# A two-layer diffusion backbone on one core: prescribed TensorE order at three places, unread products in two waits, later norm transposes inside the projection

## The chip, the cores and the metric

The kernel runs as one program on one core of one Trainium2 chip. The metric is device microseconds of one execution; a figure for a kernel is the median over several executions. PE is TensorE (PEld its weight loads), DVE is VectorE, ACT is ScalarE, POOL is GpSimd, SP is SyncE.

## The reference, cut to what matters

The kernel takes 512 latent tokens of width 1024 and 256 context tokens through two layers. Layer 0 mixes by attention and a Fourier transform, layer 1 by a conformer convolution; both end in a gated FFN with a small convolution. Each part is preceded by an RMS norm that is modulated by shift and scale vectors computed from the condition `c`.

```python
sh1, sc1, g1, sh2, sc2, g2 = ada_params(c, w_ada[i], b_ada[i])   # silu(c) @ w + b
h_lat = modulate(rmsnorm(x_lat, g_mix[i]), sh1, sc1)
o_lat, _ = hybrid_mixer(h_lat, h_ctx, ...)      # layer 0
o_lat = conformer_conv(h_lat, ...)              # layer 1: glu, dwconv 31, layernorm, silu, @ w_pw2
x_lat = x_lat + g1 * o_lat
h = modulate(rmsnorm(x_lat, g_ffn[i]), sh2, sc2)
x_lat = x_lat + g2 * conv_ffn(h, w_up[i], w_fdw[i], b_fdw[i], w_down[i])
```

All of it is float32. The kernel writes each operand as a high and a low part, and each product of two matrices as three TensorE products (high by high, low by high, high by low).

## The kernel before, in words

**Products.** `mm3` issues the three products (L224, L225, L226). Weights come in chunks of 128x1024: a transfer into `st`, ACT casts the high part `whi` (L196), DVE subtracts it for the low part `wlo` (L197). `Stream` holds five such pairs and two `st`; all transfers of this part are issued by SP in program order.

**Order.** The program text is handed to a scheduler that fixes one order for each engine before the program runs. On the chip every engine works through its own list in that order, so an instruction that waits holds up all behind it on the same engine. `issue_after(ins)` tells the scheduler that what follows may stand only behind `ins` on its list.

**Projection of layer 0 (`load_and_project`).** The input features come in eight groups `kt` of 128. For each, `modulate(kt)` makes `tmp = xnT * modA + modS` on DVE (L561), ACT casts the high part of `h` (L290), DVE subtracts the low one (L291). Then PE adds 12 products of 128x256 into the key/value accumulators (two banks, B) and 12 of 128x512 into the query accumulators (D). `modS` and `modA` come from the condition, two feature groups (a quarter) at a time: `Quarter.product` (L383, eight products with 32 output rows), a copy out of the bank by ACT (L385), and `Quarter.columns` (L391, four products that turn rows into columns). The quarter for `kt` 2 and 3 stands in the text behind `kt` 0 (product) and `kt` 1 (columns), and so on. From `kt` 4 on the context's parts are added (`hc`, L566 on ACT), and `project(0)` starts the Fourier branch (24 products of 128x512 into another bank).

**Heads (`heads_and_fourier`).** When the key/value sums are complete, ACT copies and squares them (L695, L696), DVE reduces, POOL takes a root (L287), DVE scales and rotates, PE transposes; the same for four tiles of queries.

**Attention.** For each tile of 128 queries and key/value group, four score products per head (L813), maximum on DVE (L815), exponential on ACT (L818), transposes (L830) and products with the values (L835). `fill()` runs one step of a filler: the condition's products for later parts (`Block.product`, L340), sixteen PE records in a half block.

**Tails.** In each FFN the last two chunks of the down projection are added for four token tiles `t`; then `residual` (L455, L456 on DVE), and, if a norm follows, `fin(t)`: square sum (ACT L485), root (DVE, POOL), scaling (DVE L487), and for a pair of tiles the transposes `features` (PE L472), shift and scale (ACT L477) and the split of `h` (DVE L479, L480). The next part begins with products over the first 256 tokens (`first_blocks`).

**End of the conformer.** After the fourth quarter of the convolution's inverse transform, DVE sums up the layer norm's statistics and normalises four tiles `ytm` (L1203); PE transposes them feature group by feature group (L1207, eight groups of four), ACT and DVE make `h`, and `token_major("pw2", ...)` multiplies.

Of the kernel before, what the change touches and what calls it, by code (L numbers as in the profile page):

```python
# [17 lines left out]
P = 128  # L18
# [203 lines left out]
def mm3(nc, out, lhs, rhs, start, stop):  # L222
    (lh, ll), (rh, rl) = lhs, rhs
    nc.tensor.matmul(out, lhsT=lh, rhs=rh, start=start, stop=False)  # L224
    nc.tensor.matmul(out, lhsT=lh, rhs=rl, start=False, stop=False)  # L225
    nc.tensor.matmul(out, lhsT=ll, rhs=rh, start=False, stop=stop)  # L226


@with_exitstack
def tile_hybrid_backbone(ctx: ExitStack, tc: tile.TileContext, x_in, ctx_in, vecs_in, gains_in, cond_in, condT_in, wada, wnat,  # L230
# [124 lines left out]

    turn = []

    def in_turn(dst, src):

        with tc.issue_after(turn[-1]) if turn else nullcontext():  # L360
            turn.append(nc.sync.dma_start(dst, src).ins)

    class Quarter:

# [13 lines left out]
        def product(self):  # L378
            g = bank()
            kts = range(KT) if self.qd == 0 else (6, 7, 4, 5, 2, 3, 0, 1)  # L380
            for n, kt in enumerate(kts):
                o = 32 * (kt % 4)
                nc.tensor.matmul(g[o : o + 32, :], lhsT=cT[:, kt, :], rhs=self.st[kt // 2][:, kt % 2, :], start=n < 4, stop=n >= 4)  # L383
            self.gs = tmp()
            nc.scalar.copy(self.gs, g)  # L385

        def columns(self):

            b = bank()
            for k in range(4):  # L390
                nc.tensor.matmul(b[:, 2 * k : 2 * k + 2], lhsT=self.gs[:, k * P : (k + 1) * P], rhs=sel, start=True, stop=True)  # L391
            return b[:, 0:8].rearrange("p (j k r) -> p j k r", j=2, k=2)

    def in_every_row(col, dst, halves=(0, 1)):
# [41 lines left out]
    def chain(*gens):  # L436
        for g in gens:
            yield from g
# [86 lines left out]
    def load_and_project(gain, keep, pre):  # L525
# [21 lines left out]
                else:  # L547
                    nc.vector.tensor_copy(o, i)

        def modulation(cols):  # L550

            raw = cols.columns()
# [46 lines left out]
        quarters[1].load(4)  # L599
        for t in range(TT):  # L600
            x_rows(t)
        quarters[0].product()
        modulation(quarters[0])
        stream.fill(3)
        quarters[2].load(4)
# [16 lines left out]
        for kt in range(KT):  # L622
            modulate(kt)
            stream.fill()
            wq = stream.get(("q", kt // 2))
            wk = stream.get(("kv", kt // 4))
            rq = tuple(w[:, (kt % 2) * 512 : (kt % 2 + 1) * 512] for w in wq)
            rk = rks[kt] = tuple(w[:, (kt % 4) * 256 : (kt % 4 + 1) * 256] for w in wk)
            if kt == 0:
                for kb in (K0, K1):  # L630
                    nc.tensor.matmul(kb, lhsT=zero, rhs=rq[0], start=True, stop=False)
            for t in range(TT):
                mm3(nc, kv_ps[t], hsl(h, kt, t * P, (t + 1) * P), rk, False, kt == KT - 1 and t % 2 == 1)
            for t in range(TT):
                mm3(nc, q_ps[t], hsl(h, kt, t * P, (t + 1) * P), rq, kt == 0, kt == KT - 1)
            if kt % 2 == 0 and kt < 6:
                quarters[kt // 2 + 1].product()
            if kt == 0:
                quarters[3].load(4)
            if kt % 2 == 1 and kt < 6:  # L640
                modulation(quarters[kt // 2 + 1])
            if kt == 3:
                for t in range(2):
                    ctx_rows(xcs[t], t)
                rope = chunk_tile()[:, 0:512].rearrange("p (a t d) -> p a t d", a=2, t=TT)
# [156 lines left out]
    def attention(qT, kk, vv, ap, fill):  # L802
        units = [(t, kv) for t in range(TT) for kv in range(NKV)]

        def scores(t, kv):
            ps_ = []
            for g in range(GRP):
                hd = kv * GRP + g
                s = bank2()
                lq = qT[:, hd, t * P : (t + 1) * P]  # L810
# [71 lines left out]
    def mixer():  # L882
        A2, S2 = mods[0]
        with ExitStack() as tables:
# [4 lines left out]
            with sbuf("qkv") as qkv:  # L889
# [6 lines left out]
                with sbuf("att") as ap:  # L896
# [21 lines left out]
                    filler = sums()  # L918
                    run(filler)

                    def fill():
                        stream.fill(stream.loaded + next(ahead))
                        run(filler)

                    attention(qT, kk, vv, ap, fill)
# [5 lines left out]
    def ffn(l, filler, filler1, mods, out_dram=None):  # L931
        nd = NF // 2
        with sbuf(nm("ff")) as fp:
# [88 lines left out]
                fin = finisher(fp, *mods)  # L1022
            gs = [gsplit(2 * (nd - 2) + i) for i in range(4)]
            ws = [stream.get(("dn", l, 1, nd - 2 + i)) for i in range(2)]
            for t in range(TT):
                for i in range(4):
                    mm3(nc, acc[t], tuple(u[:, t * P : (t + 1) * P] for u in gs[i]), tuple(u[:, (i % 2) * 512 : (i % 2 + 1) * 512] for u in ws[i // 2]), False, i == 3)
                residual(t, 1, acc[t], gate2, out_dram)
                if t == TT - 1:
                    for i in range(2):  # L1030
                        stream.release(("dn", l, 1, nd - 2 + i))
                if mods is not None:
                    fin(t)


    def conformer(filler, mods):
        with sbuf("cf") as cf, ExitStack() as inner:
# [57 lines left out]
            def conv_quarter(q):  # L1095
# [43 lines left out]
                def inverse(pt, bt):  # L1139
                    if bt == 0:  # L1140
                        mm3(nc, acc[pt], tuple(u[:, 4, pt * P : (pt + 1) * P] for u in iv), zs[0], True, False)
                    for o in range(2):
                        mm3(nc, acc[pt][:, o * 256 : o * 256 + 256], tuple(u[:, 2 * o + bt, pt * P : (pt + 1) * P] for u in iv),
                            tuple(u[:, o * 256 : o * 256 + 256] for u in zs[1 + bt]), False, bt == 1 and o == 1)

                for z in ((0, 0), (1, 0), (0, 1), (1, 1)):
                    inverse(*z)
                for pt in range(2):
                    ys = tmp(256)
                    nc.scalar.copy(ys, acc[pt][:, 256:512])  # L1150
# [164 lines left out]
```

## Time and profile before

| | |
|---|---|
| Median of 3 executions | 1201.29 us (1201.06 to 1203.15) |
| The profiled execution | 1202.3 us, of which the span of the core is 1200.5 us |
| Busy share of the span | PE 96 %, PEld 80 %, DVE 64 %, ACT 43 %, POOL 9 % |
| Mean granted clock of TensorE | 0.99 of full speed |

The span runs from the first to the last instruction; 1.8 us lie around it. A granted clock of 1.00 is the level of 2.4 GHz, 0.50 that of 1.2 GHz. Idle time is written behind the instruction that ended it, with the releaser.

### The profile page before, as it was taken

Reading aid. Unit: us, or ns where it says so; the run is one execution under the profiler, and the core shown is the slowest. Engines: PE = TensorE matmul, PEld = TensorE weight load, DVE = VectorE, ACT = ScalarE, POOL = GpSimd, SP = SyncE. Lnnn points to the kernel's source line nnn. Section 1 sums busy time; section 2 is a strip of 40 time slices with the busy share of each in tenths; the row PEclk is TensorE's granted clock in tenths of the full one; section 3 lists DMA queues with packets and bytes.
Section 4 is the critical chain, followed back from the end, with each engine's and each line's share of the span. In section 5 each row is a group of like instructions: output and inputs, shape, how many; then the busy total and the mean of one; then the engine's idle time right before and its main releaser. Section 6 shows DMA issues by size and latency. Waiting matters only on the chain.

```text
span 1200.5 us, 15245 instructions
## 1 busy us (share of the span) xinstructions
PE 1158.5 (96%) x5849; PEld 963.6 (80%) x5849; DVE 769.6 (64%) x1198; ACT 521.3 (43%) x789; POOL 105.0 (9%) x107
## 2 busy tenths in 40 slices
PE   6998899999999999999999999799999999999998
PEld 4787577889888888888888888688888888888886
DVE  4569688475956667676745875846695555555563
ACT  4555677345434343434433353444544343434341
POOL 0234555000000000000001310000000000000000
PEclk9999899999999999999999999999999999999999
DMA  9642333122644545453624642012262333332230
GB/s 365 250 149 88 141 141 124 53 79 72 218 159 158 171 145 172 150 188 123 209 88 163 204 153 72 22 53 86 85 215 88 93 101 98 96 101 93 97 114 35
DMA packets 43832, 156.41 MB, mean 130 GB/s; under 512 B 5008, under 2 KB 5520, under 8 KB 43504
## 3 DMA queue, kind: packets, MB, share of 16 engines
q1 hardware_dynamic: 42192, 149.51, 36.7%
q0 software_dynamic: 1120, 5.54, 1.3%
q8 instruction: 46, 0.75, 0.2%
q10 hardware_dynamic: 448, 0.39, 0.1%
q14 instruction: 26, 0.21, 0.1%
HBM read 153.33 MB, written 2.10 MB: 129 GB/s over the span
## 4 chain that ended last, share of the span: by engine, by line
PE 86%; DVE 8%; ACT 3%; issue 2%; DMA 2%; POOL 0%; SPq 0%; ACTq 0%; DVEq 0%; POOLq 0%
PE B L224 19%; PE B L225 19%; PE B L226 19%; PE D L224 7%; PE D L225 7%; PE D L226 7%; PE B L835 2%; DVE wlo L197 1%; DMA st<-in_wall_dram 1%; PE B L830 1%; PE D L813 1%; PE B L340 1%; DVE tiny L815 1%; ACT whi L196 1%; PE B L383 1%
## 5 line engine op out<-in xcount | busy, mean ns | idle before, releaser
L197 DVE TENSOR_TENSOR wlo<-st,whi 128x1024 fp32r<-128x1024 f32 x174 | 212.7, 1224 | 229.8 <-ACT whi L196 229.3
L225 PE MATMUL B<-h,whi 128*128 128x512 f32 (+1 forms) x880 | 321.1, 368 | 0.0
L226 PE MATMUL B<-h,wlo 128*128 128x512 f32 (+1 forms) x880 | 319.2, 367 | 0.0
L224 PE MATMUL B<-h,whi 128*128 128x512 f32 (+1 forms) x880 | 313.0, 368 | 3.6 <-DVE h L479 3.6
L196 ACT CAST whi<-st 128x1024 fp32r<-128x1024 f32 x174 | 182.8, 1052 | 213.9 <-PE B L225 136.7
L225 PEld LDWEIGHTS B<-h,whi 128*128 128x128 f32 x880 | 166.6, 189 | 26.8
L226 PEld LDWEIGHTS B<-h,wlo 128*128 128x128 f32 x880 | 166.4, 189 | 26.6
L224 PEld LDWEIGHTS B<-h,whi 128*128 128x128 f32 x880 | 161.6, 189 | 31.5 <-DVE h L479 5.0
L290 ACT CAST g<-g 128x512 fp32r<-128x512 f32 x88 | 54.7, 622 | 166.3 <-DVE g L958 88.2
L291 DVE TENSOR_TENSOR g<-g,g 128x512 fp32r<-128x512 f32 x88 | 60.5, 688 | 53.0 <-ACT g L290 51.3
L287 POOL TENSOR_TENSOR tiny<-tiny,mhalf 128x1 f32<-128x1 f32 (+3 forms) x26 | 21.1, 812 | 607.5 <-DVE tiny L286 606.4
L224 PE MATMUL D<-whi,g 128*128 128x512 f32 x176 | 68.5, 389 | 0.0
L225 PE MATMUL D<-wlo,g 128*128 128x512 f32 x176 | 68.5, 389 | 0.0
L224 PE MATMUL B<-whi,g 128*128 128x512 f32 x176 | 68.5, 389 | 0.0
L225 PE MATMUL B<-wlo,g 128*128 128x512 f32 x176 | 68.5, 389 | 0.0
L226 PE MATMUL D<-whi,g 128*128 128x512 f32 x176 | 68.5, 389 | 0.0
L415 DVE SCALAR_TENSOR_TENSOR sa<-sa,scb 128x1024 f32<-128x1024 f32 x56 | 66.4, 1220 | 2.2 <-ACT scb L308 1.8
L226 PE MATMUL B<-whi,g 128*128 128x512 f32 x176 | 66.2, 389 | 0.0
L948 ACT ACTIVATE tmp<-B,vecs 128x512 f32<-128x512 f32 x84 | 64.7, 773 | 0.0
L950 DVE SCALAR_TENSOR_TENSOR tmp<-B,vecs,tmp 128x511 f32<-128x511 f32 x84 | 62.7, 749 | 2.4
L949 DVE SCALAR_TENSOR_TENSOR tmp<-B,vecs,tmp 128x511 f32<-128x511 f32 x84 | 62.4, 744 | 2.9 <-ACT tmp L948 2.9
L956 ACT ACTIVATE tmp<-tmp 128x512 f32<-128x512 f32 x44 | 27.8, 631 | 82.4 <-DVE tmp L950 82.2
(243 smaller groups left out, 1816.3 us busy)
## 6 DMA issues: line engine op xcount, KB each, us to landing
st<-in_wall_dram SPq DMA_DIRECT2D x174, 512.0 KB, 3.5
sa<-in_wada_dram SPq DMA_DIRECT2D x56, 512.0 KB, 4.4
sa<-in_wnat_dram SPq DMA_DIRECT2D x18, 512.0 KB, 5.9
wn<-in_wnat_dram SPq DMA_DIRECT2D x16, 512.0 KB, 8.3
sx<-in_wnat_dram SPq DMA_DIRECT2D x6, 512.0 KB, 3.5
x<-in_x_dram SPq DMA_DIRECT2D x4, 512.0 KB, 5.2
dft<-in_dft_dram POOLq DMA_DIRECT2D x2, 1024.0 KB, 6.9
out_dram<-x SPq DMA_DIRECT2D x8, 256.0 KB, 2.0
```

Of the source, the lines that this page charges most:

```text
L196: nc.scalar.copy(hi, st)
L197: nc.vector.tensor_tensor(out=lo, in0=st, in1=hi, op=ALU.subtract)
L224: nc.tensor.matmul(out, lhsT=lh, rhs=rh, start=start, stop=False)
L225: nc.tensor.matmul(out, lhsT=lh, rhs=rl, start=False, stop=False)
L226: nc.tensor.matmul(out, lhsT=ll, rhs=rh, start=False, stop=stop)
L290: nc.scalar.copy(hi, src)
L291: nc.vector.tensor_tensor(out=lo, in0=src, in1=hi, op=ALU.subtract)
L415: nc.vector.scalar_tensor_tensor(out=st, in0=st, scalar=1.0, in1=cur["c"], op0=ALU.mult, op1=ALU.mult, accum_out=acc[:, kt : kt + 1])
L948: nc.scalar.activation(out=y, in_=b, func=AF.Identity, scale=w[:, 1:2], bias=vec(f"bfdw{l}", i))
L949: nc.vector.scalar_tensor_tensor(out=y[:, 1:SEQ], in0=b[:, 0 : SEQ - 1], scalar=w[:, 0:1], in1=y[:, 1:SEQ], op0=ALU.mult, op1=ALU.add)
L950: nc.vector.scalar_tensor_tensor(out=y[:, 0 : SEQ - 1], in0=b[:, 1:SEQ], scalar=w[:, 2:3], in1=y[:, 0 : SEQ - 1], op0=ALU.mult, op1=ALU.add)
L956: nc.scalar.activation(out=sa, in_=ya, func=AF.Silu)
```

## The change

Four things are done. First, in the projection, three products into a bank that nobody reads (`keep_busy`) stand in two waits of PE at the start, and `columns` of quarters 1 to 3 is tied behind the last key/value product of `kt` 1, 3 and 5. Second, attention runs one step of the filler, without asking for weights, ahead of the third head's scores of the first unit. Third, the last chunks of both FFNs are put in the strict order of the tiles. Fourth, sixteen products that nobody reads stand behind the last inverse transform of the conformer, and the norm's transposes for feature groups 4 to 7 are put among the products of `pw2` instead of ahead of them.

```diff
+    def keep_busy(n, lhs, rhs, last):
+        with behind(last):
+            junk = bank()
+            for _ in range(n):
+                nc.tensor.matmul(junk, lhsT=lhs, rhs=rhs, start=True, stop=True)
...
-        def columns(self):
+        def columns(self, last):
             b = bank()
             for k in range(4):
-                nc.tensor.matmul(b[:, 2 * k : 2 * k + 2], lhsT=self.gs[:, k * P : (k + 1) * P], rhs=sel, start=True, stop=True)
+                with behind(last):
+                    nc.tensor.matmul(b[:, 2 * k : 2 * k + 2], lhsT=self.gs[:, k * P : (k + 1) * P], rhs=sel, start=True, stop=True)
...
-        quarters[0].product()
+        keep_busy(1, ident, xnT[:, 0, :], quarters[0].product())
         modulation(quarters[0])
...
             if kt == 0:
                 for kb in (K0, K1):
-                    nc.tensor.matmul(kb, lhsT=zero, rhs=rq[0], start=True, stop=False)
+                    ins = nc.tensor.matmul(kb, lhsT=zero, rhs=rq[0], start=True, stop=False).ins
+                keep_busy(2, ident, xnT[:, 0, :], ins)
...
             if kt % 2 == 1 and kt < 6:
-                modulation(quarters[kt // 2 + 1])
+                modulation(quarters[kt // 2 + 1], last)
...
             for g in range(GRP):
+                if (t, kv, g) == (0, 0, 2):
+                    fill(0)
...
+            last = None
             for t in range(TT):
-                for i in range(4):
-                    mm3(nc, acc[t], ...)
+                with behind(last):
+                    for i in range(4):
+                        ins = mm3(nc, acc[t], ...)
+                last = ins
                 residual(t, 1, acc[t], gate2, out_dram)
...
+                if q == 3:
+                    spare = iv[0].rearrange("p k n -> p (k n)")
+                    keep_busy(16, spare[:, 0:P], spare[:, 0:512], last)
...
-            for kt in range(KT):
+            def norm_T(kt):
                 b = bank()
...
+            def ahead():
+                for kt in range(KT):
+                    if kt + 4 < KT:
+                        norm_T(kt + 4)
+                    run(filler, 1)
+                    yield
+            for kt in range(4):
+                norm_T(kt)
-            token_major("pw2", range(KT), gate1, finisher(xp, *mods), filler, 1)
+            token_major("pw2", range(KT), gate1, finisher(xp, *mods), chain(ahead(), filler), 1)
```

The program adds 19 products and removes none; transfers, and SP's order of issuing them, are the same. What moves is the order on the engines. The numbers behind the names are buffers; lines of the changed kernel stand some 11 to 24 lines further down. The first place is PE at the start of the projection, in the kernel before, from the condition's product for quarter 1 (L383) on:

```order
L383 MATMUL B_315<-wn_146,cT 32x512 x2
L383 MATMUL B_315<-wn_144,cT 32x512 x2
L383 MATMUL B_315<-wn_142,cT 32x512 x2
L383 MATMUL B_315<-wn_140,cT 32x512 x2
L391 MATMUL B_362<-sels,tmp_324 128x2 x4
L224 MATMUL B_283<-whi_134,h_82 128x256
L225 MATMUL B_283<-wlo_135,h_82 128x256
L224 MATMUL B_284<-whi_134,h_82 128x256
L225 MATMUL B_284<-wlo_135,h_82 128x256
```

And in the changed kernel, from the end of the products of `kt` 1 on (L404 is `columns`, L394 `product`):

```order
L226 MATMUL D_283<-whi_128,h_83 128x512
L226 MATMUL D_284<-whi_128,h_83 128x512
L224 MATMUL D_284<-whi_128,h_82 128x512
L225 MATMUL D_284<-wlo_129,h_82 128x512
L226 MATMUL D_284<-whi_128,h_83 128x512
L404 MATMUL B_367<-sels,tmp_329 128x2 x4
L394 MATMUL B_409<-wn_265,cT 32x512 x2
L394 MATMUL B_409<-wn_263,cT 32x512 x2
L394 MATMUL B_409<-wn_261,cT 32x512 x2
L394 MATMUL B_409<-wn_259,cT 32x512 x2
L224 MATMUL B_285<-whi_134,h_82 128x256
L225 MATMUL B_285<-wlo_135,h_82 128x256
```

The columns of quarter 1 stood between `kt` 0 and `kt` 1; they now stand behind all of `kt` 1, and the product of quarter 2, which stood behind `kt` 2 and 3, follows at once, ahead of `kt` 2.

The second place is DVE at the same time, in the kernel before, from the modulation of `kt` 1 (`tmp_334`) to that of `kt` 3 (`tmp_415`); `tmp_376` is that of `kt` 2, `wlo_266` and `wlo_272` are the low parts of weight chunks 3 and 4:

```order
L561 TENSOR_SCALAR tmp_334<-xnT,modA,modS 128x512
L197 TENSOR_TENSOR wlo_252<-st_253,whi_251 128x1024
L291 TENSOR_TENSOR h_83<-tmp_334,h_82 128x512
L555 TENSOR_TENSOR modS<-B_362,vecs 128x4
L556 TENSOR_TENSOR modA<-B_362,vecs 128x4
L557 TENSOR_TENSOR modA<-modA,base 128x4
L561 TENSOR_SCALAR tmp_376<-xnT,modA,modS 128x512
L291 TENSOR_TENSOR h_83<-tmp_376,h_82 128x512
L197 TENSOR_TENSOR wlo_266<-st_267,whi_265 128x1024
L197 TENSOR_TENSOR wlo_272<-st_273,whi_271 128x1024
L286 TENSOR_SCALAR tiny_455<-tiny_452 128x1
L536 TENSOR_SCALAR xn_451<-xc_277,tiny_453 128x1024
```

In the changed kernel `tmp_381` is the modulation of `kt` 2, and `wlo_268` and `wlo_274` are chunks 3 and 4:

```order
L197 TENSOR_TENSOR wlo_254<-st_255,whi_253 128x1024
L574 TENSOR_SCALAR tmp_339<-xnT,modA,modS 128x512
L291 TENSOR_TENSOR h_83<-tmp_339,h_82 128x512
L197 TENSOR_TENSOR wlo_268<-st_269,whi_267 128x1024
L568 TENSOR_TENSOR modS<-B_367,vecs 128x4
L569 TENSOR_TENSOR modA<-B_367,vecs 128x4
L570 TENSOR_TENSOR modA<-modA,base 128x4
L197 TENSOR_TENSOR wlo_274<-st_275,whi_273 128x1024
L574 TENSOR_SCALAR tmp_381<-xnT,modA,modS 128x512
L574 TENSOR_SCALAR tmp_420<-xnT,modA,modS 128x512
L286 TENSOR_SCALAR tiny_460<-tiny_457 128x1
L291 TENSOR_TENSOR h_83<-tmp_381,h_82 128x512
```

The modulation of `kt` 2 stood ahead of both chunks, and stands behind both now. On ACT the high part of `h` for `kt` 2 likewise moved behind the casts of chunks 3 and 4, the square sum of the first context tile and the copy of quarter 2.

The third place is DVE at the tail of the first FFN, in the kernel before: `tmp` is the gated sum of a tile (tile 0, then 1), `tiny` the root's argument, `xs` the scaled tile:

```order
L197 TENSOR_TENSOR wlo_5428<-st_5429,whi_5427 128x1024
L455 TENSOR_TENSOR tmp_5464<-B_5015,gate_621_2797 128x512
L455 TENSOR_TENSOR tmp_5487<-B_5016,gate_621_2797 128x512
L456 TENSOR_TENSOR x<-x,tmp_5464 128x512
L456 TENSOR_TENSOR x<-x,tmp_5487 128x512
L286 TENSOR_SCALAR tiny_5471<-tiny_5468 128x1
L487 TENSOR_SCALAR xs_5467<-x,tiny_5469 128x1024
L286 TENSOR_SCALAR tiny_5494<-tiny_5491 128x1
L487 TENSOR_SCALAR xs_5490<-x,tiny_5492 128x1024
```

And in the changed kernel:

```order
L197 TENSOR_TENSOR wlo_5433<-st_5434,whi_5432 128x1024
L468 TENSOR_TENSOR tmp_5469<-B_5020,gate_623_2802 128x512
L469 TENSOR_TENSOR x<-x,tmp_5469 128x512
L468 TENSOR_TENSOR tmp_5492<-B_5021,gate_623_2802 128x512
L286 TENSOR_SCALAR tiny_5476<-tiny_5473 128x1
L469 TENSOR_TENSOR x<-x,tmp_5492 128x512
L500 TENSOR_SCALAR xs_5472<-x,tiny_5474 128x1024
L286 TENSOR_SCALAR tiny_5499<-tiny_5496 128x1
L500 TENSOR_SCALAR xs_5495<-x,tiny_5497 128x1024
```

The residual of tile 0 stood behind the gated sum of tile 1, and now stands ahead of it.

## Rows read from the trace of the kernel before

**Rows 1.** The page, part 4: the chain that ended last, by engine.

```profile
PE 86%; DVE 8%; ACT 3%; issue 2%; DMA 2%; POOL 0%; SPq 0%; ACTq 0%; DVEq 0%; POOLq 0%
```

**Rows 2.** Windows (us): per engine busy us (x instructions), then granted clock, DMA share, GB/s.

```profile
20.00:22.00 2.00, 2.00 (x6) 1.63 (x7) 2.00 (x4) 0.66 (x1) 0.00 (x0) 0.50 1.01 365
...
57.00:60.00 3.00, 3.00 (x11) 2.53 (x10) 2.42 (x5) 3.00 (x8) 0.00 (x0) 0.50 0.11 42
...
255.00:264.00 9.00, 7.71 (x47) 6.41 (x45) 6.33 (x13) 6.07 (x10) 0.56 (x1) 1.00 0.35 118
...
634.00:637.00 3.00, 3.00 (x15) 2.98 (x15) 3.00 (x11) 1.30 (x3) 0.00 (x0) 0.50 0.78 257
...
778.00:782.00 4.00, 3.48 (x15) 3.09 (x16) 2.29 (x4) 0.15 (x1) 0.16 (x1) 0.50 0.00 0
```

**Rows 3.** Timeline of PE, projection and one L399 group: start, busy, what, idle before.

```profile
16.89 1.05 PE L391 MATMUL B<-sels,tmp 128*128 128x2 f32 x8 [0.73 <-ACT tmp L385]
...
19.76 1.22 PE L224 MATMUL D<-whi,h 128*128 128x512 f32 x2 [1.20 <-ACT h L290]
...
25.46 1.92 PE L383 MATMUL B<-wn,cT 128*32 128x512 f32 x16
...
29.03 0.36 PE L224 MATMUL B<-whi,h 128*128 128x256 f32 x1
...
33.30 0.28 PE L224 MATMUL B<-whi,h 128*128 128x256 f32 x1
...
58.24 0.42 PE L224 MATMUL B<-whi,h 128*128 128x256 f32 x1
...
156.18 1.95 PE L399 MATMUL B<-ident,tiny 128*128 128x128 f32 x16
```

**Rows 4.** Chain of waits, one piece: start, duration, 128x512 product.

```profile
64.43 0.23 PE D L225
```

**Rows 5.** Timeline of ACT, projection stage.

```profile
32.75 1.05 ACT L196 CAST whi<-st 128x1024 fp32r<-128x1024 f32 x1 [0.18 <-DMA st<-in_wall_dram]
...
34.02 1.06 ACT L534 ACTIVATE xn<-xc 128x1024 f32<-128x1024 f32 x1 [0.22 <-DMA xc<-in_ctx_dram]
...
54.48 2.08 ACT L566 ACTIVATE tmp<-xcT,modS,modA 128x256 f32<-128x256 f32 x4
...
56.46 0.61 ACT L290 CAST h<-tmp 128x512 fp32r<-128x512 f32 x1
...
73.70 0.39 ACT L696 ACTIVATE tmp<-B 128x256 f32<-128x256 f32 x1
```

**Rows 6.** Timeline of DVE, projection stage and the head stage behind it.

```profile
32.60 2.46 DVE L197 TENSOR_TENSOR wlo<-st,whi 128x1024 fp32r<-128x1024 f32 x2 [1.00 <-ACT whi L196]
...
77.18 0.17 DVE L668 TENSOR_SCALAR tiny<-tiny 128x8 f32<-128x8 f32 x1 [1.77 <-POOL tiny L287]
...
113.37 0.69 DVE L291 TENSOR_TENSOR p<-D,p 128x512 fp32r<-128x512 f32 x1
```

**Rows 7.** Timeline of PE, start of attention.

```profile
123.74 1.65 PE L813 MATMUL D<-kk,qT 128*128 128x512 f32 x4 [2.56 <-ACT P L818]
...
141.96 1.46 PE L340 MATMUL B<-sa,cT 128*32 128x512 f32 x10
```

**Rows 8.** Timeline of PE, between the mixer and the first FFN.

```profile
260.93 0.51 PE L224 MATMUL B<-h,whi 128*128 128x256 f32 x2 [0.71 <-DVE h L479]
```

**Rows 9.** Timeline of PE, between the first FFN and the conformer.

```profile
631.01 0.88 PE L472 MATMUL D<-ident,xs 128*128 128x128 f32 x6 [1.04 <-DVE xs L487]
...
633.49 0.71 PE L224 MATMUL B<-h,whi 128*128 128x256 f32 x2 [0.16 <-DVE h L479]
```

**Rows 10.** Timeline of DVE, the same place.

```profile
624.74 1.29 DVE L455 TENSOR_TENSOR tmp<-B,gate 128x512 f32<-128x512 f32 x2 [3.29 <-PE B L226]
...
630.88 2.35 DVE L197 TENSOR_TENSOR wlo<-st,whi 128x1024 fp32r<-128x1024 f32 x2
```

**Rows 11.** Timeline of PE, end of the conformer's convolution.

```profile
778.18 1.11 PE L1207 MATMUL B<-ident,ytm 128*128 128x128 f32 x4 [5.17 <-DVE ytm L1203]
```

More of the change, by code (lines that the diff above doesn't have):

```diff
@@ L225, in mm3 @@
     nc.tensor.matmul(out, lhsT=lh, rhs=rl, start=False, stop=False)
-    nc.tensor.matmul(out, lhsT=ll, rhs=rh, start=False, stop=stop)
+    return nc.tensor.matmul(out, lhsT=ll, rhs=rh, start=False, stop=stop).ins
 @with_exitstack
@@ L356, in tile_hybrid_backbone, with behind @@
     turn = []
+    def behind(ins):
+        return nullcontext() if ins is None else tc.issue_after(ins)
     def in_turn(dst, src):
@@ L382, in product @@
                 o = 32 * (kt % 4)
-                nc.tensor.matmul(g[o : o + 32, :], lhsT=cT[:, kt, :], rhs=self.st[kt // 2][:, kt % 2, :], start=n < 4, stop=n >= 4)
+                ins = nc.tensor.matmul(g[o : o + 32, :], lhsT=cT[:, kt, :], rhs=self.st[kt // 2][:, kt % 2, :], start=n < 4, stop=n >= 4).ins
             self.gs = tmp()
             nc.scalar.copy(self.gs, g)
-        def columns(self):
+            return ins
+        def columns(self, last):
             b = bank()
             for k in range(4):
-                nc.tensor.matmul(b[:, 2 * k : 2 * k + 2], lhsT=self.gs[:, k * P : (k + 1) * P], rhs=sel, start=True, stop=True)
+                with behind(last):
+                    nc.tensor.matmul(b[:, 2 * k : 2 * k + 2], lhsT=self.gs[:, k * P : (k + 1) * P], rhs=sel, start=True, stop=True)
             return b[:, 0:8].rearrange("p (j k r) -> p j k r", j=2, k=2)
@@ L548, in rows_T, with modulation @@
                     nc.vector.tensor_copy(o, i)
-        def modulation(cols):
-            raw = cols.columns()
+        def modulation(cols, last=None):
+            raw = cols.columns(last)
             k0 = 2 * cols.qd
@@ L630, in load_and_project @@
                 for kb in (K0, K1):
-                    nc.tensor.matmul(kb, lhsT=zero, rhs=rq[0], start=True, stop=False)
+                    ins = nc.tensor.matmul(kb, lhsT=zero, rhs=rq[0], start=True, stop=False).ins
+                keep_busy(2, ident, xnT[:, 0, :], ins)
             for t in range(TT):
-                mm3(nc, kv_ps[t], hsl(h, kt, t * P, (t + 1) * P), rk, False, kt == KT - 1 and t % 2 == 1)
+                last = mm3(nc, kv_ps[t], hsl(h, kt, t * P, (t + 1) * P), rk, False, kt == KT - 1 and t % 2 == 1)
             for t in range(TT):
@@ L919, in mixer, with fill @@
                     run(filler)
-                    def fill():
-                        stream.fill(stream.loaded + next(ahead))
+                    def fill(weights=1):
+                        if weights:
+                            stream.fill(stream.loaded + next(ahead))
                         run(filler)
@@ L1024, in ffn @@
             ws = [stream.get(("dn", l, 1, nd - 2 + i)) for i in range(2)]
+            last = None
             for t in range(TT):
-                for i in range(4):
-                    mm3(nc, acc[t], tuple(u[:, t * P : (t + 1) * P] for u in gs[i]), tuple(u[:, (i % 2) * 512 : (i % 2 + 1) * 512] for u in ws[i // 2]), False, i == 3)
+                with behind(last):
+                    for i in range(4):
+                        ins = mm3(nc, acc[t], tuple(u[:, t * P : (t + 1) * P] for u in gs[i]), tuple(u[:, (i % 2) * 512 : (i % 2 + 1) * 512] for u in ws[i // 2]), False, i == 3)
+                last = ins
                 residual(t, 1, acc[t], gate2, out_dram)
@@ L1142, in inverse @@
                     for o in range(2):
-                        mm3(nc, acc[pt][:, o * 256 : o * 256 + 256], tuple(u[:, 2 * o + bt, pt * P : (pt + 1) * P] for u in iv),
+                        last = mm3(nc, acc[pt][:, o * 256 : o * 256 + 256], tuple(u[:, 2 * o + bt, pt * P : (pt + 1) * P] for u in iv),
                             tuple(u[:, o * 256 : o * 256 + 256] for u in zs[1 + bt]), False, bt == 1 and o == 1)
+                    return last
                 for z in ((0, 0), (1, 0), (0, 1), (1, 1)):
-                    inverse(*z)
+                    last = inverse(*z)
+                if q == 3:
+                    spare = iv[0].rearrange("p k n -> p (k n)")
+                    keep_busy(16, spare[:, 0:P], spare[:, 0:512], last)
                 for pt in range(2):
```

## The prediction

> **What bounds the kernel now.** I read the page's chain first: PE holds 86 % of it, DVE 8 % [rows 1]. So this is a kernel whose end follows PE, except in a few places, and the question at each place that the change touches is whether PE waits there and for whom. The windows come next: they show the granted clock at 0.50 in four of these places (20 to 22, 57 to 60, 634 to 637 and 778 to 782 us), and at 1.00 in a fifth, 255 to 264, although PE was busy for only 7.71 of its 9 us [rows 2]. The timelines of PE, ACT and DVE then say who is waited for [rows 3, 5 to 11]. From about 150 us on PE has almost no idle time until the places named below, so a shift before that time reaches the end in full. Less than 0.2 % (2.4 us) can hardly be told from no change in this kernel.
>
> **The start.** The first unread product stands in the wait of 0.73 us ahead of the columns of quarter 0 [rows 3]. It is an fp32 product of 512 columns. No such one is in the trace; eight of 128 columns (16 records) took 1.95 us, the last one's tail included, so four times 0.22, about 0.89 us, is my estimate; below, it can't be under the 0.23 us of a short one [rows 3, 4]. It overruns the wait by 0.15. Two more stand in the wait of 1.20 us ahead of `kt` 0 and end near 20.2 instead of 19.76: 0.45 late. In return the clock, now at 0.50 in 20 to 22 us [rows 2], should stay up: `kt` 0 takes 5.7 us up to 25.46, where `kt` 1 takes 4.27 (29.03 to 33.30) [rows 3]. `kt` 0 ends near 24.4, about 1.0 us earlier.
>
> **The columns behind `kt` 1, 3, 5.** Here I replayed the engines' lists row by row with the durations above. The product of quarter 1 (1.92 us) now runs 24.45 to 26.4, and `kt` 1 follows without its columns: from 27.55, when ACT has copied the quarter and cast `h`, to 31.7; columns (1.05) to 32.7, product of quarter 2 to 34.6. So far PE gains 1.5 us. Then `kt` 2 needs `h`, and this is late. On DVE the modulation of quarter 1 stands behind the low part of chunk 3 and the modulation of `kt` 2 behind that of chunk 4. Those chunks wait for transfers: ACT casts chunk 4 at 32.75, and DVE makes the two low parts from 32.60 in 2.46 us [rows 5, 6]; SP issues in the same order as before, so I let them land at the same time. The two chunks and the modulation give `tmp` near 35.9; on ACT the cast stands behind the context's square sum (from 34.02, waiting for a transfer) [rows 5] and the copy of quarter 2. `kt` 2 starts near 36.7 instead of 33.30 [rows 3]: a new wait of 2.1 us. `kt` 2 and 3 end at 45.2, the columns of quarter 2 at 46.2; sixteen transposes, with two free banks between PE, ACT and DVE, reach 48.5; `kt` 4 to 53.0, product of quarter 3 to 54.95. Behind it on ACT stand its copy (like the cast of the same shape, 0.61) and four context modulations (2.08) ahead of the cast of `h` (0.61) [rows 5]: `kt` 5 starts at 58.2. Before, it started at 58.24 [rows 3], but with the columns of quarter 3 and six products of `project(0)` done, for which it found time in these waits. In the new order eighteen products of `project(0)` stand ahead of the last key/value product, where six stood: the columns (1.05) and 18 x 0.23 us [rows 4] come on top, with 0.2 for two more context products and 0.4 for a half-clock stretch that now follows the wait of 3.2 us. So the key/value sums are complete near 79.1, not 73.4.
>
> **What is late next.** ACT squares the sums (73.70), DVE reduces, POOL takes the root, and at 77.18 DVE starts a stretch without a gap over 0.5 us to 113.37 [rows 5, 6]: rotations, splits, weight chunks, the same instructions in both kernels. That stretch, and not PE, feeds attention. With sums 5.7 us later it starts near 83.0, and attention **5.8 us later**. PE itself is only 3 us late at this point. Bounds for the whole projection: if both new waits vanished because `h` came in time, PE would keep the waits that the columns cost before and gain some 3; if the clock also falls at `kt` 2, another 1.2 is lost: -3 to +7. I take +5.8, since every wait in it comes from the order of the rows.
>
> **Attention.** The step of filler is asked for ahead of the third scores, but on PE's list the first half block still stands behind that score; the wait of 2.56 us remains [rows 7]. What moves is the second half block, from 141.96 (the last ten of its sixteen records: 1.46 us there) to between later scores, where PE waits for ACT anyhow. It may have to wait for its own transfers there, with scores queued behind it. Gain 1.5 at most, loss up to 1; I take **-0.5**.
>
> **Tail of the mixer.** The first transposes of the scaled tiles move in front of the last products; the wait of 0.71 us at 260.93 [rows 8] should go: **-0.7**, between 0 and -1.3 with a second, shorter wait behind it.
>
> **Tail of the first FFN.** Tile 0 is complete 2.7 us (twelve products of 0.23) earlier, tile 1 as before. DVE did both tiles' sums together at 624.74 (1.29 us), then both residuals [rows 10]. Now tile 0's are done before tile 1 is complete, and tile 1's two instructions end near 626.15 instead of 627.2; ACT has squared tile 0 by then, and `xs` of tile 1 is ready near 629.0, 2 us earlier. The wait of 1.04 for it at 631.01 goes [rows 9]; chunks that stood on DVE from 630.88 (2.35 us) [rows 10] start at 629.0, and the first product of the next part at 631.8 instead of 633.49: -1.7. If the clock does not fall, up to another 1.7: 3.4 us of the time behind it ran at half [rows 2]. The waits shrink from 2.0 to 0.9 us; around 260 us the clock stood at 1.00 with 1.3 of waits. I take **-2.7**, between -1.7 and -3.4. The second FFN's tail gives nothing: its last product stays where it is.
>
> **End of the conformer.** Sixteen products of 0.23 are 3.7 us within a wait of 5.17 [rows 11]; they end at 776.5, and the first transposes start at 778.18 as before, since DVE sets this. At half clock four of them take 1.11 us, at full six take 0.88 [rows 9, 11]. Two groups stand behind the last tile of DVE, so **-1.0** if the clock stays up, 0 if not. Without the cover of that wait the products would cost 3.7. Transposes for groups 4 to 7: on PE's list only the last group really moves, some 26 products; PE is busy either way: 0.
>
> **Sum.** 5.8 - 0.5 - 0.7 - 2.7 - 1.0 = +0.9 us on the profiled execution's 1202.3 (span 1200.5, 1.8 around it). That execution lies 1.0 above the median; on the median of 1201.3 the forecast is 1202.2 us.
>
> **Rivals.** *The clock falls wherever a wait remains* (slower). The new wait of 2.1 us at `kt` 2 costs 1.2, the FFN's tail keeps its half clock (-1.7 instead of -2.7), the conformer's transposes gain nothing. For it: before `kt` 0 waits of 0.73 and 1.20 sufficed [rows 2, 3]. Against it: the window around 260. Sum +0.9 + 1.2 + 1.0 + 1.0 = +4.1, 1205.4 us. It decides if all three places show 0.50. The Trainium skill, TensorE: Matmul & The Clock Gate, Part 4 (PE-mode transpose), says that transposes do not count as PE being busy in the way products do; by that rule the conformer's clock falls among them, its term is 0 and the sum +1.9 where the rows give +0.9. No row here separates transposes from waits.
>
> *The projection's waits do not appear* (faster). If chunks 3 and 4, the context tile and the copies come early enough that `kt` 2 and `kt` 5 start without the new waits, the projection gives between 0 and -3 instead of +5.8: the sum is then -5 to -8, 1193 to 1196.5 us. For it: with the columns out of the way PE reaches the product of quarter 2 5 us earlier, which frees the buffers for SP's next transfers. Against it: the transfers waited for are issued ahead of those. It decides if `kt` 2 starts before 34.6.
>
> *The delay stays PE's 3 us* and does not grow to DVE's 5.8, because DVE's stretch has slack that its list does not show: -1.9, 1199.4 us.
>
> **How the numbers follow.** The forecast and its neighbours (1200 to 1204): 0.40. The clock rival and other losses: 0.30. DVE's slack: 0.12, most of it within 0.2 %. The absent waits: 0.18. The range 1195.5 to 1206 leaves out the better half of the absent waits and what goes beyond the clock rival. Faster by over 0.2 % (under 1198.9): 0.18 and a part of the slack, 0.25; slower (over 1203.7): the clock rival and the upper edge of the forecast, 0.35; within: 0.40.
>
> **What would show it.** Right: `kt` 2 starts near 36.7 and `kt` 5 near 58.2; key/value sums complete near 79; attention's first long wait near 129; the first FFN's transposes without a wait for `xs`; clock 1.00 at 778 to 782, shifted. Wrong: a start of `kt` 2 before 35, or DVE reaching its stretch before 80. A wait of PE for DMA in the first unit of attention would add to the loss.

## The result and the profile after

The changed kernel takes 1209.27 us (median of six executions) against 1201.95 (six). One of the six ran at 1310.7 us with a mean granted clock of 0.85; without it the median is 1207.02, and the ratio of the others to before is 1.0058, 95 % interval 1.0047 to 1.0070, so about 7 us slower. The forecast was 1202.2 us and no change. The five lie at two levels: three at 1206.3 to 1207.0, with mean granted clocks of 0.994 to 0.996, and two at 1211.5 and 1212.1, with 0.990 and 0.989. The profiled execution took 1206.83 us with a span of 1205.1: 4.6 above the span of before. On its page the chain still belongs to PE, but DMA has 3 % of it where it had 2:

```profile
PE 86%; DVE 6%; DMA 3%; ACT 3%; issue 1%; POOL 1%; SPq 0%; ACTq 0%; DVEq 0%
```

**Projection.** PE's timeline, where `kt` 1, `kt` 2 and `kt` 5 start and the columns of quarter 3 stand:

```profile
27.50 0.39 PE L224 MATMUL B<-whi,h 128*128 128x256 f32 x1 [1.25 <-ACT h L290]
36.42 0.39 PE L224 MATMUL B<-whi,h 128*128 128x256 f32 x1 [1.83 <-ACT h L290]
58.37 0.38 PE L224 MATMUL B<-whi,h 128*128 128x256 f32 x1 [3.18 <-ACT h L290]
64.12 0.95 PE L404 MATMUL B<-sels,tmp 128*128 128x2 f32 x8
```

These are the waits that were forecast (36.7 and 58.2), within 0.3 us; before, `kt` 2 started at 33.30 without one [rows 3]. DVE's and ACT's timelines show what held them:

```profile
34.03 1.23 DVE L197 TENSOR_TENSOR wlo<-st,whi 128x1024 fp32r<-128x1024 f32 x1
35.18 1.00 DVE L574 TENSOR_SCALAR tmp<-xnT,modA,modS 128x512 f32<-128x512 f32 x2
81.77 0.17 DVE L682 TENSOR_SCALAR tiny<-tiny 128x8 f32<-128x8 f32 x1 [1.77 <-POOL tiny L287]
117.16 0.69 DVE L291 TENSOR_TENSOR p<-D,p 128x512 fp32r<-128x512 f32 x1
```

```profile
32.73 1.04 ACT L196 CAST whi<-st 128x1024 fp32r<-128x1024 f32 x1 [0.21 <-DMA st<-in_wall_dram]
35.75 1.14 ACT L290 CAST h<-tmp 128x512 fp32r<-128x512 f32 x2
55.74 2.07 ACT L579 ACTIVATE tmp<-xcT,modS,modA 128x256 f32<-128x256 f32 x4
57.72 0.60 ACT L290 CAST h<-tmp 128x512 fp32r<-128x512 f32 x1
```

Chunk 4's low part at 34.03 stands ahead of the modulation of `kt` 2 at 35.18, and the four context modulations at 55.74 ahead of the cast for `kt` 5. DVE's long stretch starts at 81.77 and ends at 117.16, where before it was 77.18 and 113.37 [rows 6]: 4.6 late at its start, 3.8 at its end.

**Attention.** PE's timeline in the first unit:

```profile
127.54 1.65 PE L829 MATMUL D<-kk,qT 128*128 128x512 f32 x4 [2.56 <-ACT P L834]
134.71 1.05 PE L340 MATMUL B<-sx,cT 128*32 128x512 f32 x4 [0.70 <-DMA sx<-in_wnat_dram]
139.54 3.21 PE L340 MATMUL B<-sa,cT 128*32 128x512 f32 x12 [2.60 <-DMA sa<-in_wnat_dram]
```

The long wait for ACT is the same 2.56 as before [rows 7]. New are two waits for transfers, 3.3 us together, ahead of the first four and the last twelve records of the second half block. DVE and ACT get no scores meanwhile (ACT sits idle for 5.6 us), and behind the second wait the clock is down (0.83 over 136 to 146 us):

```profile
20.00:22.00 2.00, 2.00 (x11) 1.64 (x10) 1.93 (x3) 0.66 (x1) 0.00 (x0) 1.00 0.98 322
57.00:60.00 3.00, 1.63 (x9) 1.44 (x10) 1.36 (x3) 1.94 (x5) 0.00 (x0) 1.00 0.00 0
136.00:146.00 10.00, 7.41 (x40) 4.03 (x39) 4.24 (x8) 3.81 (x8) 3.76 (x3) 0.83 0.69 259
634.00:640.00 6.00, 4.78 (x31) 3.85 (x30) 4.87 (x10) 4.37 (x7) 0.00 (x0) 1.00 0.30 93
```

These windows give the granted clock third from the end of the row. At the start, at 57 and at the first FFN's tail it is 1.00, where it was 0.50 [rows 2].

**Tails.** Between mixer and FFN the wait for DVE did not go: two of 0.71 [rows 8] and 0.58 us became one of 1.49. From the product at 269.83 to the end of the first FFN everything is 6.2 us late. Then the FFN's tail gains: the first transposes run without a wait for `xs`, and the next part starts at 638.51, 5.0 late, at full clock, so that it is 3.7 late by 641. PE's timeline, the two places:

```profile
269.83 0.50 PE L224 MATMUL B<-h,whi 128*128 128x256 f32 x2 [1.49 <-DVE h L492]
637.96 0.66 PE L485 MATMUL D<-ident,xs 128*128 128x128 f32 x4 [1.19 <-ACT tmp L490]
638.51 0.50 PE L224 MATMUL B<-h,whi 128*128 128x256 f32 x2
```

**Conformer.** At its entry PE has waits of 0.46 and 0.36 us that were not there. It reaches the last inverse transform and the transposes behind it 4.8 us late (783.00 for 778.18 [rows 11]) and is 4.5 late at the first products behind the transposes:

```profile
723.55 0.38 PE L1130 MATMUL B<-ws,vt 96*128 96x256 f32 x1 [0.46 <-ACT V L1133]
724.41 0.38 PE L224 MATMUL B<-eo,fw 128*128 128x256 f32 x1 [0.36 <-DVE tmp L1081]
777.66 3.81 PE L372 MATMUL B<-iv 128*128 128x512 f32 x16
783.00 0.66 PE L1231 MATMUL B<-ident,ytm 128*128 128x128 f32 x4 [1.53 <-DVE ytm L1227]
```

### The profile page after: what moved, and what is told of

It reads as the page before. It is cut to its first block, busy times and chain, and to the rows that moved or that the text cites. A ratio compares the mean times of both kernels' runs of the same rounds, so it can differ in the third digit from the quotient of the medians.

```text
span 1205.1 us, 15290 instructions
## 1 busy us (share of the span) xinstructions
PE 1161.4 (96%) x5871; PEld 963.9 (80%) x5871; DVE 769.5 (64%) x1198; ACT 520.9 (43%) x789; POOL 106.6 (9%) x107
## 3 DMA queue, kind: packets, MB, share of 16 engines
q1 hardware_dynamic: 42192, 149.51, 36.4%
## 4 chain that ended last, share of the span: by engine, by line
PE 86%; DVE 6%; DMA 3%; ACT 3%; issue 1%; POOL 1%; SPq 0%; ACTq 0%; DVEq 0%
PE B L224 19%; PE B L225 19%; PE B L226 19%; PE D L225 6%; PE D L224 6%; PE D L226 6%; DMA st<-in_wall_dram 2%; PE B L851 2%; PE B L846 1%; DVE wlo L197 1%; PE D L829 1%; PE B L340 1%; ACT whi L196 1%; PE D L485 1%; PE B L412 1%
## 5 line engine op out<-in xcount | busy, mean ns | idle before, releaser
L224 PEld LDWEIGHTS B<-h,whi 128*128 128x128 f32 x880 | 161.0, 189 | 31.1 <-DVE h L492 4.6
```

## The experiments

My theory after this profile: the tied columns delay the projection (P), the early filler step makes PE wait for transfers in attention (F), and the rest gains. Rivals stand with each run. The first run repeats the changed kernel, and the next three undo one or both. The runs were made on three chips, each beside the kernel before on the same chip.

**e1_again**: the changed kernel, no edit.

> The changed kernel once more, unaltered. Its executions lay at two levels, 1206.3 to 1207.0 and 1211.5 to 1212.1 us. Theory C (granted clock): the two levels differ by stretches at half clock behind the new waits at kt 2 and kt 5; a profile of the upper level shows a granted clock of 0.50 at 36 to 40 or 58 to 62 us, where the profiled execution showed 1.00, and its attention starts 3 to 5 us later. Rival: the levels come from transfers; the clock is the same in both and a wait for DMA is longer. Median between 1206.5 and 1212.

Measured: 1206.91 us (1205.8 to 1210.4), ratio 1.0050 (1.0037 to 1.0063). Its profile, the same lists and waits, shows a clock below 1.00 behind the wait at `kt` 5, which is again 3.18 us, and DVE's stretch ends at 118.36, 1.2 later than in the first profile. The first row is of the first profile, the others are of this one:

```profile
56.00:62.00 6.00, 3.63 (x22) 3.28 (x23) 1.36 (x3) 2.94 (x7) 0.00 (x0) 1.00 0.00 1
56.00:62.00 6.00, 3.90 (x19) 3.68 (x20) 1.36 (x3) 2.66 (x7) 0.00 (x0) 0.78 0.00 0
62.00:66.00 4.00, 4.00 (x26) 3.53 (x25) 0.85 (x2) 1.25 (x3) 0.00 (x0) 0.90 0.00 0
```

So theory C holds in kind: the same program has its clock lowered at this place in one execution and not in another. At `kt` 2 the clock stayed up in both. The mean granted clock of the executions says the same of the two levels: it is 0.005 lower in the upper one, and 0.005 of 1205 us is 6 us of full-speed time (an estimate), against 5 us between the levels. In e1 too the fastest execution (1205.8) has 0.995 and the slowest (1210.4) 0.990. So the levels go with the clock; 1.2 us of it lie at `kt` 5, and where an execution of the upper level loses the rest was not profiled.

**e2_no_fill, e3_no_columns, e4_neither**: one or both of these edits.

```diff
-                if (t, kv, g) == (0, 0, 2):
-                    fill(0)
```

```diff
-                modulation(quarters[kt // 2 + 1], last)
+                modulation(quarters[kt // 2 + 1])
```

> The changed kernel without the early step of the filler in attention. Theory F: the step brings 3.3 us of waits for DMA in the first unit, with the scores queued behind, and costs 2.5 to 3 us net; without it 1203.5 to 1204.5 us at the lower level. Rival P: the projection's delay of 3.8 us and nothing else makes the loss, the waits for DMA are covered; then it stays at 1206 to 1207.

> The changed kernel with the columns of quarters 1 to 3 free again, the early filler step kept. Theory P: the columns cost the 3.8 us of the projection and the upper level; without them 1202 to 1203 us, one level only. Theory F alone: the loss stays, 1206 or more, because PE waits for DMA all the same; attention starting earlier would even make the wait for the transfers longer by part of the 3.8 us.

> The changed kernel without the early filler step and without the tied columns: the unread products at both places, the tiles' strict order in the FFNs and the later norm transposes stay. P and F together: start -1.0, first FFN's tail -2.5, conformer -0.3 from the trace of after, so about 1197.5 to 1198.5 us, faster than before. If the gain at the first FFN's tail is not real (half clock there by chance) it is 1200 to 1201.

Measured on the same chip (before: 1201.18):

| run | median us | ratio to before (95 %) |
|---|---|---|
| e1_again | 1206.91 | 1.0050 (1.0037 to 1.0063) |
| e2_no_fill | 1205.27 | 1.0035 (1.0023 to 1.0047) |
| e3_no_columns | 1197.90 | 0.9970 (0.9958 to 0.9981) |
| e4_neither | 1196.14 | 0.9962 (0.9950 to 0.9974) |

The columns cost 9.0 us with the filler step (1206.91 - 1197.90) and 9.1 without, so "the filler alone" falls. The step costs 1.6 to 1.8, less than I expected; the intervals of the two pairs overlap, so these medians do not exclude "the projection alone" by themselves. Without both, the change is faster than before by 5 us. DVE's stretch starts at 74.00 in e4, 7.8 us ahead of the changed kernel and 3.2 ahead of before:

```profile
74.00 0.17 DVE L682 TENSOR_SCALAR tiny<-tiny 128x8 f32<-128x8 f32 x1 [1.77 <-POOL tiny L287]
110.48 0.69 DVE L291 TENSOR_TENSOR p<-D,p 128x512 fp32r<-128x512 f32 x1
```

**e5_tail_only, e6_conformer_only, e7_start_only**: the kernel before with one of the other parts: `with behind(last)` in the FFN; `keep_busy(16, ...)` and `ahead()`; `keep_busy(1, ...)` and `keep_busy(2, ...)`, each as in the diff of the change.

> The kernel before with the strict order of the tiles in the FFN tails alone. Theory: the first FFN's tail gains 2.5 us as in the trace of after (1.7 by the earlier xs, the rest by the clock) and the entry of the conformer, whose order on PE changes with it, gives back 1.0; 1199.5 to 1200 us. Rival: the clock's share came from the other changes; then 1200.5 to 1201.

> The kernel before with the sixteen unread products and the later norm transposes alone. Theory: 0.3 us gained as in the trace of after, so 1200.9, same as before. Rival: the products keep the clock up through the transposes and the start of the projection behind them, 1.0 us, 1200.2.

> The kernel before with the three unread products at the start alone. Theory: no half clock at 19 to 23 us, and PE's later start at kt 0 costs 0.45: 1.0 to 1.7 us gained where attention starts, 1199.5 to 1200.2. Rival: DVE's stretch behind the projection does not start earlier and nothing is gained, 1201.2.

Measured against 1200.75: the tail 1199.28, 0.9984 (0.9975 to 0.9993); the conformer 1200.33, 0.9995 (0.9986 to 1.0004); the start 1200.07, 0.9991 (0.9982 to 1.0000). The tail gains 1.5, as the theory had it. The conformer's 0.4 is not clear of nothing, and its interval holds the rival's 1.0 too. The start gains 0.7, at the edge of its interval. Together that is 2.6 by medians, and e4 gained 5.0; by the ratios it is 3.6 and 4.6, and that difference lies within the intervals.

The profiles show how far a single one can be trusted. Up to DVE's stretch the lists of e5, e6 and e12 are those of before, and their stretches end at 111.78, 113.07 and 112.03, where before shows 113.37: one list varies by 1.6 us, and before's profile is the latest of the four. So the 3.2 us of e4 are in part the luck of that profile. And the three products at the start do more than keep the clock up: with them the scheduler puts the product of quarter 2 ahead of `kt` 2 even where no columns are tied. In the kernel before it stood behind `kt` 2 alone, at 37.58 us, and not behind `kt` 2 and 3 as the part on the change has it; and the wait of 0.71 us that stood there ahead of its columns is gone. PE's timeline in e7:

```profile
32.16 1.92 PE L394 MATMUL B<-wn,cT 128*32 128x512 f32 x16
38.30 0.95 PE L404 MATMUL B<-sels,tmp 128*128 128x2 f32 x8
```

**e8_columns_1, e9_columns_3, e10_columns_5**: e4 with one quarter's columns tied.

```diff
-                modulation(quarters[kt // 2 + 1])
+                modulation(quarters[kt // 2 + 1], last if kt == 1 else None)
```

(3 and 5 in the other two.)

> The run without the filler step and without tied columns (1196.1 us), with the columns of quarter 1 alone tied behind kt 1. Theory: the loss of the tied columns, 9 us in the runs so far, is mostly that of quarter 3 (18 products of project(0) ahead of the last key/value product, a wait of 3.2 us at kt 5); quarter 1 alone costs the late h of kt 2, about 2 us: 1198 to 1198.5. Rival: the wait at kt 2 is the root of all of it, 1202 or more.

> The run without the filler step and without tied columns (1196.1 us), with the columns of quarter 2 alone tied behind kt 3. Quarter 1 alone brought it to 1200.0. Theory: each tie sets kt's features behind its own wait and moves the rest of the list; the three together cost 9, so quarter 2 costs 1 to 3: 1197 to 1199. Rival: quarter 1's wait is what counts and quarter 2 and 3 add nothing by themselves: 1196.

> The same run with the columns of quarter 3 alone tied behind kt 5. Theory: PE waits some 3 us for h at kt 5 with nothing to do, since columns and the first products of project(0) stand behind, and twelve more of these stand ahead of the last key/value product: 3 to 5 us, 1199.5 to 1201. Rival as above: 1196.

Measured: 1199.97 us, 0.9992 (0.9983 to 1.0000); 1196.22, 0.9964 (0.9951 to 0.9976); 1200.52, 0.9999 (0.9990 to 1.0008). Against e4 quarter 1 costs 3.8, quarter 2 nothing, quarter 3 4.4: together 8.3 of the 9. That quarter 1's wait is the root of all falls. For quarter 1 the trace of e8 gives the edit itself only part: attention starts 1.4 us later than in e4, and that stays so up to 715 us. The rest of the 4.0 between the two profiles is the granted clock at two places where the lists are the same, 1.4 us behind 716 and 1.3 us among the transposes behind 777. e8 first, then e4 at the same work:

```profile
716.00:720.00 4.00, 3.88 (x16) 3.64 (x17) 2.36 (x6) 0.71 (x2) 0.00 (x0) 0.57 0.49 155
777.00:781.00 4.00, 2.81 (x13) 2.42 (x13) 1.44 (x3) 1.11 (x3) 0.00 (x0) 0.60 0.00 0
```

```profile
714.00:718.00 4.00, 3.64 (x22) 3.14 (x22) 3.40 (x7) 1.42 (x4) 0.00 (x0) 1.00 0.54 160
774.00:778.00 4.00, 2.53 (x18) 2.19 (x19) 2.34 (x4) 2.07 (x5) 0.00 (x0) 1.00 0.00 0
```

Whether the tie brings these falls about or the two executions differ by chance is not shown.

**e13_columns_5_ctx, e14_neither_ctx**: which of two things costs at quarter 3, the wait for `h` or the eighteen products of `project(0)` ahead of the last key/value product (before and in e4: six). In e10 and in e4 the context modulations are put behind the cast for `kt` 5, which the helper hands over as `cur["h5"]`:

```diff
+            with behind(cur["h5"]):
-            nc.scalar.activation(out=c32, in_=xcT[:, kt, :], ...)
+                nc.scalar.activation(out=c32, in_=xcT[:, kt, :], ...)
...
-            if kt >= 4:
-                ctx_part(2 * (kt - 4))
-                ctx_part(2 * (kt - 4) + 1)
+            for c in {5: (0, 1, 2, 3), 6: (4, 5), 7: (6, 7)}.get(kt, ()):
+                ctx_part(c)
```

> The run with quarter 3's columns alone tied (1200.5 us), with the four context modulations of kt 4 put behind the cast of h for kt 5 on ACT. Theory W: the wait for h at kt 5 makes the loss; it shrinks from 3.2 to about 1.1 us and the time falls by 2 us, to 1198.5. Rival O: the order of project(0) ahead of the last key/value product makes it; the wait shrinks, the time stays at 1200 to 1200.5.

> The same edit on the run without filler step and without tied columns (1196.1 us). Both theories: PE does not wait for h at kt 5 there, so the edit changes nothing, 1195.5 to 1196.7; if it alone moves the time by over 1 us, the run above is read against this one.

Measured: 1197.54 us, 0.9967 (0.9956 to 0.9979), and 1196.76, 0.9966 (0.9955 to 0.9978). PE's timeline at the start of `kt` 5, e10 and then e13:

```profile
55.16 0.39 PE L224 MATMUL B<-whi,h 128*128 128x256 f32 x1 [3.18 <-ACT h L290]
```

```profile
53.72 0.39 PE L224 MATMUL B<-whi,h 128*128 128x256 f32 x1 [1.53 <-ACT h L290]
```

With the wait at 1.53 the loss of quarter 3 shrinks from 4.4 to 0.8 (e13 against e14, which have the same edit). That speaks for W; but on e13's list twelve products stand ahead of the last key/value product, not eighteen, so O is not out: the wait is 1.65 us shorter, and six products are 1.4 of the 3.0 us won.

**e11_fill_no_load, e12_fill_only**: the filler step. e11 leaves out the transfers of the second half block (its products read the first half's chunks again); it is e3 with

```diff
-                            if n + 1 < len(todo):
+                            if 0 < n and n + 1 < len(todo):
```

> The run with free columns and the early filler step (1197.9 us), in which the first block's second half does not load its four chunks and multiplies the first half's chunks instead (so gate1 is computed from half of its weights). Theory F: the step's loss is PE's wait for these transfers; without them 1195 to 1196.2 us. Rival: what costs is where the products stand among the scores; 1197.9 stays.

> The kernel before with the early filler step alone. Theory F: attention is entered as before, the transfers of the second half block come late for PE as in the trace of after, 1.5 to 3 us lost: 1202.3 to 1203.8. Rival: the step costs only where the projection is late as well; 1200.8, same as before.

Measured: 1195.62 us, 0.9962 (0.9949 to 0.9974), and 1201.22, 1.0007 (0.9998 to 1.0016). PE's timeline, e3 and then e11:

```profile
129.09 1.05 PE L340 MATMUL B<-sx,cT 128*32 128x512 f32 x4 [0.76 <-DMA sx<-in_wnat_dram]
133.82 1.91 PE L340 MATMUL B<-sa,cT 128*32 128x512 f32 x12 [2.03 <-DMA sa<-in_wnat_dram]
```

```profile
126.85 0.60 PE L340 MATMUL B<-sx,cT 128*32 128x512 f32 x2
127.29 1.45 PE L340 MATMUL B<-sa,cT 128*32 128x512 f32 x10
```

Without the transfers the waits go and the median falls by 2.3 us, to e4's level. Two things keep this from settling F. The intervals of e3 and e11 overlap. And in e11 the scheduler set the second half block right behind the first, ahead of eight score products, so its place changed too. On the kernel before the step costs 0.5, which its interval does not tell from nothing, although the same waits (1.56 and 1.99 us) stand in its profile.

The traces say more. Take the time from the end of DVE's stretch to a product behind the mixer that waits 0.7 us for `h` in every run (at 276.07 in the kernel before, 282.28 in the changed kernel). It is 165.1 us in the changed kernel and 165.8 in e1; in the eleven profiles without the step it is 161.0 to 163.4 (162.0 in e2, which differs by the step alone). With the step and free columns it is 163.8 (e3) and 163.1 (e12), and 161.2 without the transfers (e11). So beside tied columns the step's waits cost 3 to 4 us at this point, clear of the spread; by the medians of e1 and e2, 1.6 of it are left at the end. Beside free columns at most 0.4 us lie beyond the spread. One difference is on record: behind the second wait the clock is down in the changed kernel and in e1 (0.83 over 136 to 146 us in both), and it is 1.00 there in e3 and e12.

## Why the prediction was wrong

**The projection** went as replayed. Both new waits, their place and their length came out (36.4 and 58.4 for 36.7 and 58.2), and so did their mechanism: the casts and modulations stand behind chunks and context work. DVE's stretch started 4.6 us late, not 5.8, because the half clock that I had put behind the wait at `kt` 5 did not come in this execution (57 to 60 us: 1.00); in e1 and e2, where it came, it took 1.2 us for the 0.4 of the sum, and DVE's stretch started at 83.03 and 83.12, as forecast (83.0). What the columns cost in the end is more. The term holds the start's -1.0, so for the columns alone it stands for 6.8 us. The end of DVE's stretch carries that much: 117.2, 118.4 and 119.0 in the three profiles with all columns tied (the changed kernel, e1, e2), and 111.7, 110.5 and 112.2 in e3, e4 and e11, a difference of 6.7 between the means. The runs give 9.0 and 9.1; the other 2 us come behind the projection.

**The term that failed is attention's**: "Gain 1.5 at most, loss up to 1; I take -0.5". I had named the wait for the half block's own transfers and the scores behind it, and priced it at 1. From DVE's end of stretch to the FFN's start the trace loses 2.4 us (3.8 late to 6.2 late), the mixer's tail included, which was to gain 0.7 and gained nothing. That tail belongs to the step as well: its two waits became one of 1.5 to 1.8 us in the five profiles with the step and stayed two in those without it (0.71 and 0.51 in e2). So the step was forecast at -1.2, and the experiments give +1.6 to +1.8. SP issues the second half's transfers once the first half's products have freed the buffers. The last of them is issued at 132.8 us, and PE starts on it at 139.5: its time to landing, 6.7 us, stands nearly in full, since the products were moved next to the ones that free their buffers. In the old order the issues lay at 127.3 to 129.2 and the products at 141.5, twelve us behind.

**The start** was put at -1.0 within the sum. e4 shows -3.2 at DVE's stretch, against a late profile of before; e7 gives -0.7 by medians. That "waits of 0.73 and 1.20 sufficed" for the clock to fall does not hold of every execution: in e5 the same two waits left it at 1.00.

**The tail of the first FFN** came as priced in the trace (6.2 late to 3.7 late, so -2.5 for -2.7), half of it by the clock. What I did not see is 1.1 us given back between there and 771 us, most of it in two waits at the conformer's entry, where the scheduler's order moved too. The tail alone brings 1.5.

**The conformer**: -1.0 forecast, -0.3 in the trace, -0.4 by medians. The clock stayed up at first and fell 0.5 us behind the start of the transposes, so the sign "clock 1.00 at 778 to 782, shifted" did not come; and the first transposes were bound by DVE's `ytm`, not by PE.

**The rule on transposes** of the Trainium skill (TensorE: Matmul & The Clock Gate, Part 4), which the prediction set against it, would have the clock fall among them. It did fall there in the changed kernel, but behind a wait of 1.53 us too. In e4, with the same list and a wait of 1.52 at 773.24, it did not fall among the transposes at all. So no run here decides it. The changed kernel, then e4:

```profile
783.50:787.50 4.00, 2.98 (x14) 2.42 (x12) 1.61 (x3) 0.83 (x2) 0.00 (x0) 0.57 0.00 0
772.00:782.00 10.00, 7.19 (x43) 5.88 (x44) 7.22 (x13) 6.07 (x14) 1.22 (x2) 1.00 0.00 0
```

The sum of the profiled execution is 3.8 + 2.4 - 2.5 + 1.1 - 0.3 = +4.5 us for a forecast of +0.9. By the ratios the change costs 6.0 to 7.0 us, 1.5 to 2.5 more than this pair of profiles: the profiled execution of before lies 1.0 above its median, and that of the changed kernel is one of the lower level. The rival of the clock gave about the right size (+4.1) for the wrong reason: the FFN's tail kept its clock.

By the medians of the experiments the sum reads so:

| part | forecast | measured |
|---|---|---|
| start, first FFN's tail, conformer (e4 against before) | -4.7 | -5.04 |
| tied columns (e1 against e3) | +6.8 | +9.01 |
| filler step with the mixer's tail (e3 against e4) | -1.2 | +1.76 |
| all (e1 against before) | +0.9 | +5.73 |

So the gains came, the step's sign was wrong, and the columns cost 2 us more than forecast. That the gains came as forecast is in part luck: the same three parts, run singly, give 2.6 us.

What of this is shown: the columns' cost of 9 us, nearly all at quarters 1 and 3; the filler step's waits for transfers and their loss beside tied columns; that putting the context modulations behind the cast for `kt` 5 takes away most of quarter 3's cost. What stays open: how that cost divides between the wait and the six products, why the clock falls in e8 at 716 and not in e4, and where the upper level of 5 us loses its clock. The version that beats both kernels is e4, 1196.1 us: the unread products, the tiles' order and the later transposes, without tied columns and without the filler step.

## What to carry to other kernels

An instruction that is moved out of a short wait takes its consumers along. Before it is tied behind a block, list what its result feeds on every other engine, and what now stands ahead of that: here 0.7 us of waits became 2 and 3 us, with the work that used to fill them behind the tie. And work that is pulled forward into a wait must have its data: if its transfers can only start when the work just ahead frees their buffers, the whole time to landing stands in front of it (6.7 us for the last of four transfers here). A profile is one execution: the same list reached DVE's stretch 1.6 us apart in two of them, so a difference of that size between two profiles is not yet an effect of the change.

## What the runs showed of the hardware

The same wait of 3.18 us at `kt` 5 stands in four profiles. Over 56 to 62 us the granted clock was 1.00 in the changed kernel and in e10, 0.78 in e1 and 0.79 in e2. At the start the same list with the same waits of 0.73 and 1.20 us was at 1.00 in e5 and at 0.72 in e6 over 18 to 24 us (e5, then e6):

```profile
18.00:24.00 6.00, 4.80 (x30) 3.73 (x32) 3.97 (x6) 1.60 (x3) 0.00 (x0) 1.00 1.03 397
18.00:24.00 6.00, 4.80 (x17) 3.66 (x16) 4.04 (x6) 2.12 (x3) 0.00 (x0) 0.72 1.01 393
```

Whether a wait lowers the clock was thus not fixed by its length, and a term of a sum that hangs on it is uncertain by 1 us or more at each such place.

Products that nobody reads did keep the clock up. Over 20 to 22 us it was 1.00 in all twelve profiles with the three products at the start, and 0.50, 1.00, 0.50 and 0.63 in the four without them (before, e5, e6, e12). Over the four us ahead of the conformer's first transposes it was 1.00 in the twelve profiles with the sixteen products, and 0.69 to 0.85 in the four without (before, e5, e7, e12). Over the six us behind that point the wait in front is 1.5 us instead of 5.2, and the clock was still down in ten of the twelve (0.72) and at 1.00 in e4 and e11. What that is worth in time is small: 0.4 us by the medians of e6.
